# A hybrid decoder layer on one core: the GDN samples' side work queued behind the casts of the states, their decay on ScalarE and additions made wider, and key norms five columns at a time

## The chip, the core and the metric

One NeuronCore of a Trainium2 chip. The time is device microseconds for one execution of the whole program, from 512 prompt tokens and 8 sequences of 8 sample tokens to all eight outputs.

## The reference, cut

```python
def _layer(x, s_gla, s_gdn, conv_buf, ...):
    h = _rmsnorm(x, ln_g)
    proj = h @ w_in                                   # 2048 x 18480
    (q_a, k_a, v_a, lr_a, gate_a, qkv_b, beta_b, dec_b, gate_b, m_a, m_b) = split(proj)
    ...
    o_a, s_gla_new = _gla_chunked(q_a, k_a, v_a, log_alpha, s_gla)       # 4 heads, 256 x 512 states
    y_a = (rmsnorm(o_a) * silu(gate_a)) @ w_br_a
    qkv, conv_new = _causal_conv(qkv_b, conv_buf, conv_w)
    q_b, k_b, v_b = split(silu(qkv))
    q_b, k_b = _l2norm(q_b) * GDN_DK ** -0.5, _l2norm(k_b)
    o_b, s_gdn_new = _gdn_chunked(q_b, k_b, v_b, g, beta, s_gdn)         # 16 heads, 128 x 128 states
    y_b = (rmsnorm(o_b) * silu(gate_b)) @ w_br_b
    return x + (sigmoid(m_a) * y_a + sigmoid(m_b) * y_b) @ w_out, s_gla_new, s_gdn_new, conv_new

def step(s, inp):                                     # of _gdn_chunked, one chunk
    ...
    sol = triangular_solve(eye + m, [v * beta, k * beta * exp(gh)])      # -> u, w
    v_new = u - w @ s
    o = (q * exp(gh)) @ s + qk @ v_new
    s = s * exp(g_last) + k_end.T @ v_new
```

The layer runs twice, on the prompt with zero states and on the samples with states that are loaded; then a last RMSNorm. For the samples each of 16 GDN heads has eight states of 128 x 128.

## The kernel before, in words

Every projection is a row of blocks of 128 output columns over all 576 tokens. A block takes 96 matmuls on TensorE in two halves (256 prompt tokens; 256 prompt and 64 sample tokens): weights and tokens are split into a high and a low part, and three products are added. The weights of the block after the next are loaded, and those of the next are cut while a block runs: the high part `hi` by ScalarE (L249), the low part `lo` by VectorE (L252). All else is side work: generators that issue a piece, name a pause and are taken up again when TensorE's matmuls have gone on by so much (`Seq`, L41). TensorE's order is the order of writing. On the other engines the framework's scheduler orders instructions by its own estimate of when they can start; each engine then runs its queue strictly in that order. `S.marks` holds instructions behind which, on their own engine, everything is queued that a later step of side work issues; before the change it holds only the last cast of weights on ScalarE.

The change touches two places.

*The key heads* (`key_task`, L927, 16 heads, some 250 us): the key rows' squares are summed per token into `ss`, four columns of 128 tokens and one of 64 sample tokens. VectorE makes from them the write strengths and the factors of the end-of-chunk keys, and GpSimd the norms `sqk`, once for the four columns and once for the fifth (L957 to L965).

*The GDN samples* (L1515 to L1679), which run beside eleven blocks of merge gates (`mth`, L1008, is their tanh). Per head h:

- `gdn_sample_load` (L1518) loads the eight states `Sbd` (512 KB, five buffers) and the head's small tiles; the load of h + 2 is issued at the start of head h.
- `gdn_sample_prep` (L1535) cuts keys and queries into `kqp` and the states into `Shl`: high part by ScalarE (L1551), low part by VectorE (L1552), each in two halves of four states. It is issued in head h - 1, right after `zs`.
- `gdn_sample` (L1556): eight `ksq` matmuls; ScalarE copies their low-part columns to `ksqe` (L1567); eight additions on VectorE make `ks_` and `qs_`; `zs` (L1577); matmul `nps`; its copy `nns` (L1584); `kw` (ScalarE and VectorE) goes to HBM (`d_kw`, L1595).
- `gdn_sample_end` (L1600): matmul `ops`, the output `os`, its squares `jks` (L1610), its factor `rss` (L1611 to L1613, the last a power on GpSimd), its scaling by GpSimd (L1614); `kr` comes back from HBM (L1616); transpose `op2`, product with the gate, store; GpSimd spreads `kr` into `bd` (L1626); two matmuls `sps2`, after each of which VectorE updates four states in place, `Sbd * decay + sps2` (L1635); the states go out (L1638).

All DMAs are issued by SP in one queue. There, in steady work, stand per head: the states of h - 3 out, `d_kw` of h, the load of `Sbd` for h + 2, `d_ob`, `kr`, seven small loads. Five buffers mean that the load for h + 2 waits until the states of h - 3 are out.

The matmul of `sps2` for head h comes about three heads after its `ksq`; the second of its two stands, for half of the heads, just behind the `ksq` of head h + 3.

Of the kernel before, what the change touches and what calls it, by code (L numbers as in the profile page):

```python
# [7 lines left out]
F32 = mybir.dt.float32  # L8
F32R = mybir.dt.float32r
U8 = mybir.dt.uint8  # L10
AF = mybir.ActivationFunctionType
ALU = mybir.AluOpType
# [4 lines left out]
P = 128  # L17
# [3 lines left out]
TS = 64  # L21
T = TP + TS
HALVES = ((0, 256), (256, T))
NB = 8
# [3 lines left out]
EPS = 1e-6  # L28
# [75 lines left out]
def build(ctx, tc, nc, x_p, x_s, st_gla, st_gdn, st_conv, ln_g, w_in, w_al, b_al, conv_w,  # L104
# [3 lines left out]
    S = Seq(tc)  # L108
# [44 lines left out]
    halfc = cg.tile([P, 1], F32, name="halfc")  # L153
# [5 lines left out]
    def build_masks(maskb):  # L159
        G.memset(maskb, 0.0)  # L160
        mp = maskb[:, 0:P]
        G.affine_select(out=mp, in_=mp, pattern=[[1, P]], compare_op=ALU.is_ge,
                        fill=NEG, base=0, channel_multiplier=-1)
        ms2 = maskb[:, P:P + TS]
        G.affine_select(out=ms2, in_=ms2, pattern=[[1, TS]], compare_op=ALU.is_ge,
                        fill=NEG, base=0, channel_multiplier=-1)
        ms = ms2.rearrange("p (b s) -> p b s", s=LS)
        G.affine_select(out=ms, in_=ms, pattern=[[-LS, NB], [0, LS]], compare_op=ALU.is_ge,
                        fill=NEG, base=0, channel_multiplier=1)
        V.tensor_scalar(cmask, maskb, -1.0, None, ALU.is_ge)  # L170
# [6 lines left out]
    def chunks():  # L177
        return ((P, 0, 4), (TS, 4, 5))
# [748 lines left out]
    def key_task(pk, h, ext, exs, lst, ready):  # L927
# [14 lines left out]
                         bias=nghc[:, c, h:h + 1])  # L942
        A.activation(W[0:TS, TP:T], R[0:TS, TP:T], AF.Exp, bias=nghc[0:TS, 4, h:h + 1])
        yield 10.0
        ss = pk.tile([P, 5], F32, name="ssk", tag="ssk")
        jk = pk.tile([P, P], F32, name="jk", tag="jk", bufs=1)
        kp = big("kp")
        for c in range(4):
# [5 lines left out]
        A.activation(jk[0:TS], kps[0:TS, 0:P], AF.Square, accum_out=ss[0:TS, 4:5])  # L954
        tb = pk.tile([P, 5], F32, name="tb", tag="tb")
        ck = pk.tile([P, 5], F32, name="ck", tag="ck")
        for n, s, e in chunks():  # L957
            V.tensor_scalar(tb[0:n, s:e], ss[0:n, s:e], EPS, None, ALU.add)
            V.reciprocal(ck[0:n, s:e], tb[0:n, s:e])
            V.tensor_tensor(out=bti[0:n, h, s:e], in0=ck[0:n, s:e], in1=btc[0:n, s:e, h],  # L960
                            op=ALU.mult)
            V.tensor_tensor(out=ck[0:n, s:e], in0=bti[0:n, h, s:e], in1=ekc[0:n, s:e, h],
                            op=ALU.mult)
            G.tensor_tensor(out=sqk[0:n, h, s:e], in0=tb[0:n, s:e],
                            in1=halfc[0:n].broadcast_to([n, e - s]), op=ALU.pow)  # L965
        ke = pk.tile([P, 5, P], F32, name="ke", tag="ke")
        for c in range(4):
            V.tensor_scalar(ke[:, c], kp[:, c * P:(c + 1) * P], ck[:, c:c + 1], None, ALU.mult)
# [51 lines left out]
    def k_open():  # L1020
        cp_open()
        px = pool(kctx2, "px", side="right")
        lrb, dec, lrs, zt = (px.tile([32, T], F32, name="lrb"), px.tile([16, T], F32, name="dec"),
                             px.tile([96, T], F32R, name="lrs"), px.tile([P, TS], F32, name="zt"))
        SY.dma_start(dec, d_dc)
        SY.dma_start(lrb, d_lr)
        G.memset(lrs.bitcast(F32), 0.0)
        G.memset(zt, 0.0)
        pk = kst["pk"] = pool(kctx, "pk", bufs=2)
        hk = pk.tile([P, 16, 24], F32, name="hisk", bufs=1)  # L1030
        SY.dma_start(hk, d_hi[:, 16:32])
        for j in range(16):
            his[16 + j] = hk[:, j]
        kst["lst"] = (pk.tile([P, 16, 3], F32, name="lstP", bufs=1),
                      pk.tile([P, 16, 24], F32, name="lstS", bufs=1))
        kst["maskb"] = pk.tile([P, P + TS], F32, name="maskb", bufs=1)
        build_masks(kst["maskb"])
        kst["p2c"] = ExitStack()
        kst["p2"] = pool(kst["p2c"], "p2", side="right")
        ev = S.spawn(iter(()), 5.0)  # L1040
        kst["tok"] = S.spawn(token_scalars(kst["p2"], lrb, dec, lrs, zt, ev, kst["colsready"]))
# [493 lines left out]
    def gdn_sample_prep(h, loaded):  # L1535
        pe2 = est["pe2"]
        Sb, kq, vk, ua, gt = loaded

        kqp = est["kqp"][h % 2]
        kq4 = kq.rearrange("p a (j x) -> p a j x", j=2)  # L1540
        for a in range(2):
            for j in range(2):
                src = kq4[:, a, j].rearrange("p (b s) -> p b s", s=LS)
                hi, lo = (kqp[:, 512 * j + 64 * a + o:512 * j + 64 * a + o + 544].rearrange(
                    "p (b x) -> p b x", x=136)[:, :, 0:LS] for o in (0, 32))
                A.copy(hi, src)
                V.tensor_tensor(out=lo, in0=src, in1=hi.bitcast(F32), op=ALU.subtract)
        sh = pe2.tile([P, NB, 2, P], F32R, name="Shl", tag="Shl")
        for j in range(2):
            bs = slice(4 * j, 4 * j + 4)  # L1550
            A.copy(sh[:, bs, 0], Sb[:, bs])  # L1551
            V.tensor_tensor(out=sh[:, bs, 1], in0=Sb[:, bs], in1=sh[:, bs, 0].bitcast(F32),  # L1552
                            op=ALU.subtract)
        return sh

    def gdn_sample(h, loaded, sh, ahead):  # L1556
        pe, pe2 = est["pe"], est["pe2"]
# [7 lines left out]
        kj = ksq.rearrange("p (j a v) -> p j a v", j=2, a=2)  # L1565
        e = pe2.tile([P, 2, P], F32, name="ksqe", tag="ksqe", bufs=1)
        A.copy(e, kj[:, :, 1])  # L1567
        ks_ = pe2.tile([TS, P], F32, name="ks_", tag="ks_")
        qs_ = pe2.tile([TS, P], F32, name="qs_", tag="qs_")
        for out, o in ((ks_, 0), (qs_, 64)):  # L1570
            for j in range(2):
                r = slice(32 * j, 32 * j + 32)
                V.tensor_tensor(out=out[r], in0=kj[o:o + 32, j, 0], in1=e[o:o + 32, j],
                                op=ALU.add)
                V.tensor_tensor(out=out[r], in0=kj[o + 32:o + 64, j, 0], in1=out[r], op=ALU.add)
        zs = pe2.tile([TS, P], F32, name="zs", tag="zs")
        V.scalar_tensor_tensor(out=zs, in0=ks_, scalar=neghc[0:TS, 4, h:h + 1],  # L1577
                               in1=vk[:, 0], op0=ALU.mult, op1=ALU.add)
# [2 lines left out]
        np_ = chn("nps")  # L1581
        mm(np_[0:TS, 0:P], ua[:, 0], zs)
        nn = pe2.tile([TS, P], F32, name="nns", tag="nns")
        V.tensor_copy(nn, np_[0:TS, 0:P])  # L1584
        kw = pe2.tile([TS, 3, 256], F32R, name="kw", tag="kw")
        A.copy(kw[:, 0, 0:P], vk[:, 1])
        A.copy(kw[:, 2, 0:P], vk[:, 1])
# [6 lines left out]
        for j in range(2):  # L1594
            SY.dma_start(d_kw[h].rearrange("(x r) j c -> x r j c", r=3)[:, :, j],  # L1595
                         kw[32 * j:32 * j + 32].bitcast(F32))
        S.spawn(gdn_sample_end(h, loaded, nn, qs_), 3.0)
        yield 3.4

    def gdn_sample_end(h, loaded, nn, qs_):  # L1600
# [10 lines left out]
        V.tensor_scalar(rs, sqq[0:TS, h, 4:5], P * EPS, P * EPS * EPS, ALU.mult, ALU.add)  # L1611
        V.scalar_tensor_tensor(out=rs, in0=so, scalar=1.0 / P, in1=rs, op0=ALU.mult, op1=ALU.add)
        G.tensor_tensor(out=rs, in0=rs, in1=nhalf[0:TS], op=ALU.pow)  # L1613
        G.tensor_scalar(o_, o_, rs, None, ALU.mult)  # L1614
        kr = pe2.tile([96, 2, 256], F32R, name="kr", tag="kr")
        SY.dma_start(kr.bitcast(F32), d_kw[h])  # L1616
        yield 8.0
# [12 lines left out]
        for j in range(2):  # L1630
            sp = big("sps2")
            mm(sp, kr[:, j, 0:P], bd[:, j].rearrange("p g v -> p (g v)"))
            for g in range(4):
                b = j * 4 + g
                V.scalar_tensor_tensor(out=Sb[:, b], in0=Sb[:, b], scalar=elb[:, h, 4 + b:5 + b],  # L1635
                                       in1=sp[:, g * P:(g + 1) * P], op0=ALU.mult, op1=ALU.add)
            yield 1.0
        SY.dma_start(n_gdn_s[0, :, h].rearrange("b d v -> d b v"), Sb)  # L1638

# [34 lines left out]

    def m1_close():
        S.join()
        ectx.close()

    add_m(NM1, pre=m1_open, post=m1_close)  # L1679
# [338 lines left out]
```

## Time and profile before

| | |
|---|---|
| median of 3 runs | 2873.26 us (2872.47 to 2873.99) |
| the profiled execution | 2873.5 us, span 2871.8 us |
| TensorE busy | 2800.1 us (98%) |
| VectorE, ScalarE, GpSimd busy | 1758.8, 1032.6, 420.9 us (61%, 36%, 15%) |
| mean granted TensorE clock | 0.987 of full speed |

Engines are called PE (TensorE matmul), PEld (its weight loads), DVE (VectorE), ACT (ScalarE), POOL (GpSimd) and SP; SPq is SP's queue of DMA issues. Times are in us from the span's start. A matmul's duration includes its way through the array, so consecutive ones overlap; what one costs is the distance between starts. In brackets behind an instruction stands how long its engine was idle before it and what ended that. A wait for several things is put down to the last one.

### The profile page before, as it was taken

Reading aid. Unit: us, or ns where it says so; the run is one execution under the profiler, and the core shown is the slowest. Engines: PE = TensorE matmul, PEld = TensorE weight load, DVE = VectorE, ACT = ScalarE, POOL = GpSimd, SP = SyncE. Lnnn points to the kernel's source line nnn. Section 1 sums busy time; section 2 is a strip of 40 time slices with the busy share of each in tenths; the row PEclk is TensorE's granted clock in tenths of the full one; section 3 lists DMA queues with packets and bytes.
Section 4 is the critical chain, followed back from the end, with each engine's and each line's share of the span. In section 5 each row is a group of like instructions: output and inputs, shape, how many; then the busy total and the mean of one; then the engine's idle time right before and its main releaser. Section 6 shows DMA issues by size and latency. Waiting matters only on the chain.

```text
span 2871.8 us, 50272 instructions
## 1 busy us (share of the span) xinstructions
PE 2800.1 (98%) x19894; PEld 2669.6 (93%) x19894; DVE 1758.8 (61%) x3578; ACT 1032.6 (36%) x2305; POOL 420.9 (15%) x605
## 2 busy tenths in 40 slices
PE   8999999999999999999999999997799999999998
PEld 7999999989999999999999999997689888999886
DVE  7677665766568888634666666657654664533323
ACT  5444444655423232333333333333333332322222
POOL 2000000542101010101222222212210000111111
PEclk9999999999999999999999999998899999999999
DMA  6333334555653333535454444456666887644422
GB/s 165 118 114 122 126 121 140 155 176 166 171 123 80 105 102 94 146 95 141 122 136 122 126 134 122 116 147 174 171 208 198 269 289 245 185 128 125 168 75 96
DMA packets 550057, 417.33 MB, mean 145 GB/s; under 512 B 78389, under 2 KB 475397, under 8 KB 547893
## 3 DMA queue, kind: packets, MB, share of 16 engines
q1 hardware_dynamic: 549822, 414.13, 50.1%
q8 instruction: 156, 2.56, 0.4%
q14 instruction: 79, 0.65, 0.1%
HBM read 313.65 MB, written 100.40 MB: 144 GB/s over the span
## 4 chain that ended last, share of the span: by engine, by line
PE 70%; DVE 4%; issue 2%; POOL 1%; DMA 1%; ACT 1%; SPq 0%; POOLq 0%; DVEq 0%; ACTq 0%
PE mm L115 53%; PE oacc L115 7%; PE opd L115 1%; PE sps L115 1%; DVE tmp L899 1%; DVE lo L252 1%; PE ksq L115 1%; PE sp L115 1%; PE qk L115 0%; PE spd L115 0%; DVE nt L902 0%; PE ksp L115 0%; POOL bd L1626 0%; PE yp L115 0%; PE kk L115 0%
## 5 line engine op out<-in xcount | busy, mean ns | idle before, releaser
L115 PE MATMUL mm<-hh,hi 128*128 128x320 f32 (+2 forms) x3928 | 1183.8, 304 | 0.3 <-DVE qd L1241 0.3
L115 PE MATMUL mm<-hl,hi 128*128 128x320 f32 (+2 forms) x3928 | 1152.6, 296 | 0.0
L115 PE MATMUL mm<-hh,lo 128*128 128x320 f32 (+2 forms) x3928 | 1104.2, 296 | 1.2 <-DVE lo L252 0.9
L115 PEld LDWEIGHTS mm<-hh,hi 128*128 128x128 f32 x3928 | 746.6, 190 | 9.0 <-issue 3.8
L115 PEld LDWEIGHTS mm<-hl,hi 128*128 128x128 f32 x3928 | 746.0, 190 | 1.9
L115 PEld LDWEIGHTS mm<-hh,lo 128*128 128x128 f32 x3928 | 725.2, 190 | 1.9 <-DVE lo L252 1.2
L252 DVE TENSOR_TENSOR lo<-raw,hi 128x512 fp32r<-128x512 f32 x624 | 435.5, 719 | 264.6 <-ACT hi L249 263.2
L249 ACT CAST hi<-raw 128x512 fp32r<-128x512 f32 x628 | 359.4, 619 | 562.0 <-PE mm L115 460.7
L115 PE MATMUL mm<-lb,hi 128*128 128x320 f32 (+1 forms) x1024 | 211.3, 300 | 0.0
L115 PE MATMUL mm<-ra,hi 128*128 128x320 f32 (+1 forms) x1024 | 202.3, 294 | 0.0
L115 PEld LDWEIGHTS mm<-lb,hi 128*128 128x128 f32 x1024 | 165.1, 189 | 17.6 <-issue 14.9
L115 PE MATMUL oacc<-hi,m 128*128 128x512 f32 x540 | 171.1, 390 | 0.0
L115 PEld LDWEIGHTS mm<-ra,hi 128*128 128x128 f32 x1024 | 163.6, 188 | 0.0
L115 PE MATMUL mm<-lb,lo 128*128 128x320 f32 (+1 forms) x512 | 151.2, 295 | 0.0
L115 PE MATMUL mm<-ra,lo 128*128 128x320 f32 (+1 forms) x512 | 150.6, 294 | 0.0
L115 PE MATMUL mm<-tl,hi 128*128 128x288 f32 x544 | 146.8, 295 | 0.0
L115 PE MATMUL mm<-th,hi 128*128 128x288 f32 x544 | 146.7, 297 | 0.0
L899 DVE TENSOR_TENSOR tmp<-nt 128x1 f32<-128x1 f32 (+36 forms) x163 | 131.5, 807 | 3.0
L115 PEld LDWEIGHTS oacc<-hi,m 128*128 128x128 f32 x540 | 101.4, 188 | 25.2
L854 DVE SCALAR_TENSOR_TENSOR acc<-ext,cwT,acc 128x600 f32<-128x600 f32 x144 | 121.1, 841 | 0.9 <-ACT acc L852 0.6
L379 DVE TENSOR_TENSOR lo<-raw,hi 128x1024 fp32r<-128x1024 f32 x68 | 83.0, 1221 | 55.7 <-ACT hi L378 54.2
L115 PE MATMUL oacc<-lo,m 128*128 128x512 f32 x300 | 117.0, 392 | 0.0
(905 smaller groups left out, 3835.9 us busy)
## 6 DMA issues: line engine op xcount, KB each, us to landing
raw<-in_w_in SPq DMA_DIRECT2D x144, 1024.0 KB, 6.2
raw<-in_w_br_b SPq DMA_DIRECT2D x16, 1024.0 KB, 6.0
Sb<-in_state_gla SPq DMA_DIRECT2D x32, 512.0 KB, 5.8
out<-Sb SPq DMA_DIRECT2D x32, 512.0 KB, 3.1
raw<-in_w_br_a SPq DMA_DIRECT2D x16, 1024.0 KB, 6.1
raw<-in_w_out SPq DMA_DIRECT2D x16, 1024.0 KB, 5.1
Sbd<-in_state_gdn SPq DMA_DIRECT2D x16, 512.0 KB, 6.8
out<-Sbd SPq DMA_DIRECT2D x16, 512.0 KB, 3.3
```

The costliest lines, as they stand in the source:

```text
L115: PE.matmul(out, lhsT, rhs, start=start, stop=stop, **kw)
L249: hc = A.copy(hi, raw)
L252: cut = eng.tensor_tensor(out=lo, in0=raw, in1=hi.bitcast(F32), op=ALU.subtract)
L379: last_split[0] = V.tensor_tensor(out=lo, in0=src, in1=hi.bitcast(F32), op=ALU.subtract)
L854: V.scalar_tensor_tensor(out=acc, in0=ext[:, i:i + 600], scalar=cw(i), in1=acc, op0=ALU.mult, op1=ALU.add)
L899: V.tensor_tensor(out=tv, in0=nt[:, cs, c0:i], op=ALU.mult, in1=nt[:, c0:i, i:i + 1].rearrange("p j o -> p o j").broadcast_to([P, m, i - c0]))
```

## The change

Five edits. (1) `gdn_sample_prep` puts the last cast of the states on ScalarE and its low half on VectorE into `S.marks`: what later steps of side work issue on these engines is queued behind them, until the samples are done. (2) The decay of the states leaves the update: ScalarE multiplies each state in place (`gdn_sample_decay`), right after `kw`, and the update is one addition of 512 columns per `sps2`. (3) The high- and low-part columns of `ksq` are added for all 128 rows in one instruction, and the four additions of 32 rows that are left read SBUF alone. (4) The copy `nns` and the scaling of `os` go to ScalarE. (5) The key norms are handled for all five columns at once; the parts of the fifth column that no sample fills, and `ss`, are cleared beforehand by GpSimd.

```diff
-        ss = pk.tile([P, 5], F32, name="ssk", tag="ssk")
+        ss = kst["ss"][h % 2]
...
-        for n, s, e in chunks():
-            V.tensor_scalar(tb[0:n, s:e], ss[0:n, s:e], EPS, None, ALU.add)
-            V.reciprocal(ck[0:n, s:e], tb[0:n, s:e])
-            V.tensor_tensor(out=bti[0:n, h, s:e], in0=ck[0:n, s:e], in1=btc[0:n, s:e, h],
-                            op=ALU.mult)
-            V.tensor_tensor(out=ck[0:n, s:e], in0=bti[0:n, h, s:e], in1=ekc[0:n, s:e, h],
-                            op=ALU.mult)
-            G.tensor_tensor(out=sqk[0:n, h, s:e], in0=tb[0:n, s:e],
-                            in1=halfc[0:n].broadcast_to([n, e - s]), op=ALU.pow)
+        V.tensor_scalar(tb, ss, EPS, None, ALU.add)
+        V.reciprocal(ck, tb)
+        V.tensor_tensor(out=bti[:, h], in0=ck, in1=btc[:, :, h], op=ALU.mult)
+        V.tensor_tensor(out=ck, in0=bti[:, h], in1=ekc[:, :, h], op=ALU.mult)
+        G.tensor_tensor(out=sqk[:, h], in0=tb, in1=halfc.broadcast_to([P, 5]), op=ALU.pow)
...
+        kst["ss"] = [pk.tile([P, 5], F32, name=f"ssk{i}", bufs=1) for i in range(2)]
+        for t_ in kst["ss"] + [btc, ekc]:
+            G.memset(t_, 0.0)
...
-            A.copy(sh[:, bs, 0], Sb[:, bs])
-            V.tensor_tensor(out=sh[:, bs, 1], in0=Sb[:, bs], in1=sh[:, bs, 0].bitcast(F32),
-                            op=ALU.subtract)
+            S.marks["sA"] = A.copy(sh[:, bs, 0], Sb[:, bs])
+            S.marks["sV"] = V.tensor_tensor(out=sh[:, bs, 1], in0=Sb[:, bs],
+                                            in1=sh[:, bs, 0].bitcast(F32), op=ALU.subtract)
         return sh
+
+    def gdn_sample_decay(h, Sb):
+        for b in range(NB):
+            A.activation(Sb[:, b], Sb[:, b], AF.Copy, scale=elb[:, h, 4 + b:5 + b])
...
         A.copy(e, kj[:, :, 1])
+        V.tensor_tensor(out=e, in0=kj[:, :, 0], in1=e, op=ALU.add)
...
-                r = slice(32 * j, 32 * j + 32)
-                V.tensor_tensor(out=out[r], in0=kj[o:o + 32, j, 0], in1=e[o:o + 32, j],
-                                op=ALU.add)
-                V.tensor_tensor(out=out[r], in0=kj[o + 32:o + 64, j, 0], in1=out[r], op=ALU.add)
+                V.tensor_tensor(out=out[32 * j:32 * j + 32], in0=e[o:o + 32, j],
+                                in1=e[o + 32:o + 64, j], op=ALU.add)
...
-        V.tensor_copy(nn, np_[0:TS, 0:P])
+        A.copy(nn, np_[0:TS, 0:P])
...
+        gdn_sample_decay(h, Sb)
         S.spawn(gdn_sample_end(h, loaded, nn, qs_), 3.0)
...
-        G.tensor_scalar(o_, o_, rs, None, ALU.mult)
+        A.activation(o_, o_, AF.Copy, scale=rs)
...
-            for g in range(4):
-                b = j * 4 + g
-                V.scalar_tensor_tensor(out=Sb[:, b], in0=Sb[:, b], scalar=elb[:, h, 4 + b:5 + b],
-                                       in1=sp[:, g * P:(g + 1) * P], op0=ALU.mult, op1=ALU.add)
+            half_ = Sb[:, 4 * j:4 * j + 4].rearrange("p b v -> p (b v)")
+            V.tensor_tensor(out=half_, in0=sp, in1=half_, op=ALU.add)
...
         S.join()
+        S.marks.pop("sA"), S.marks.pop("sV")
```

The lines of the kernel after are some four lower than before in the key heads and one to three different in the samples (`Shl` L1550 and L1551, `nns` L1586, decay L1557, update L1637). TensorE's matmuls stand in the same order in both, and so do SP's DMAs of the samples but for the places of three around head 14.

On ScalarE before, around the casts of the states of head 11 (`jks` is that of head 10):

```order
L249 CAST hi<-raw 128x512 x4
L1610 ACTIVATE jks,sos<-os 64x128
L1586 CAST kw<-vks 64x128
L1587 CAST kw<-vks 64x128
L1551 CAST Shl<-Sbd 128x4x128 x2
L1546 CAST kqp_21683<-kqs 128x4x8 x4
L1567 COPY ksqe<-ksq 128x256
L1590 CAST kw<-nns 64x128
```

On ScalarE now, around the casts of the same states (`ksqe` and `nns` are those of head 10, `os` that of head 9):

```order
L1570 COPY ksqe<-ksq 128x256
L1545 CAST kqp_21594<-kqs 128x4x8 x4
L1617 ACTIVATE os<-os,rss 64x128
L249 CAST hi<-raw 128x512
L1004 ACTIVATE mth<-mm 128x320
L249 CAST hi<-raw 128x512 x3
L1550 CAST Shl<-Sbd 128x4x128 x2
L1586 COPY nns<-nps 64x128
L1588 CAST kw<-vks 64x128
L1589 CAST kw<-vks 64x128
L1592 CAST kw<-nns 64x128
L1593 CAST kw<-nns 64x128
```

The casts moved from behind `jks` of head 10 to ahead of its `nns`; the four `hi` and a `mth` stand ahead of them.

On VectorE before, around the low halves of the states of head 11 (`os` and the first `rss` are of head 10; the `rss` of L1611 is of head 12):

```order
L1609 TENSOR_TENSOR os<-ops,qs__23443 64x128
L1621 TENSOR_TENSOR oTs<-op_23566,gts 128x64
L1635 SCALAR_TENSOR_TENSOR Sbd<-Sbd,elb,sps_23574 128x128
L1612 SCALAR_TENSOR_TENSOR rss<-sos,rss 64x1
L1635 SCALAR_TENSOR_TENSOR Sbd<-Sbd,elb,sps_23574 128x128 x3
L252 TENSOR_TENSOR lo<-raw,hi 128x512 x2
L1588 TENSOR_TENSOR kw<-vks,kw 64x128
L252 TENSOR_TENSOR lo<-raw,hi 128x512
L1611 TENSOR_SCALAR rss<-sqq 64x1
L1552 TENSOR_TENSOR Shl<-Sbd,Shl 128x4x128 x2
```

On VectorE now, around the low halves of head 13 (`zs` and the rows behind `Shl` are of head 12, but the first Sbd is the second half of the update of head 9, the next one the first half of head 10):

```order
L1579 SCALAR_TENSOR_TENSOR zs<-ks__23673,neghc,vks 64x128
L1546 TENSOR_TENSOR kqp_21594<-kqs,kqp_21594 128x4x8 x4
L252 TENSOR_TENSOR lo<-raw,hi 128x512 x4
L1551 TENSOR_TENSOR Shl<-Sbd,Shl 128x4x128 x2
L1637 TENSOR_TENSOR Sbd<-sps_23694,Sbd 128x512
L1590 TENSOR_TENSOR kw<-vks,kw 64x128
L1594 TENSOR_TENSOR kw<-nns,kw 64x128
L1637 TENSOR_TENSOR Sbd<-sps_23775,Sbd 128x512
L1612 TENSOR_TENSOR os<-ops,qs__23674 64x128
L1614 TENSOR_SCALAR rss<-sqq 64x1
```

The low halves moved ahead of `os`, `rss` and `kw` of the head before; behind them stands the second half of the update of the head four before.

## Rows read from the trace of the kernel before

**Rows 1.** Busy time by stretches: us, busy us per engine, PEclk, DMA share, GB/s.

```profile
1600.00:1897.00 297.00, 296.56 (x2334) 290.66 (x2333) 176.59 (x459) 97.87 (x262) 66.22 (x122) 1.00 0.47 127
...
1902.00:2104.00 202.00, 165.36 (x1025) 150.36 (x1025) 148.88 (x469) 72.77 (x250) 49.34 (x56) 0.88 0.62 167
...
2131.00:2400.00 269.00, 269.00 (x1790) 242.59 (x1788) 154.12 (x276) 94.08 (x178) 10.49 (x9) 1.00 0.82 255
```

**Rows 2.** Waits from 1880 to 2130: us in total, times, longest us.

```profile
PE ksq L115 <- DVE Shl L1552: 32.0, 9, 6.6
...
ACT jks L1610 <- DVE os L1609: 18.8, 9, 4.0
...
ACT Shl L1551 <- DMA uas<-d_At: 6.2, 1, 6.2
...
PE nps L115 <- DVE zs L1577: 4.6, 4, 2.0
```

**Rows 3.** Timeline: start, us, engine, line, instruction, count, idle before it.

```profile
1942.04 1.10 PE L115 MATMUL ksq<-Shl,kqp 128*128 128x256 f32 x8
...
2043.05 0.31 ACT L1610 ACTIVATE jks<-os 64x128 f32<-64x128 f32 x1
...
2043.74 1.14 ACT L1551 CAST Shl<-Sbd 128x512 fp32r<-128x512 f32 x2
...
2044.38 2.52 POOL L1614 TENSOR_SCALAR os<-os,rss 64x128 f32<-64x128 f32 x1
...
2046.93 0.15 DVE L1611 TENSOR_SCALAR rss<-sqq 64x1 f32<-64x1 f32 x1 [0.51 <-POOL os L1614]
2047.01 3.04 DVE L1552 TENSOR_TENSOR Shl<-Sbd,Shl 128x512 fp32r<-128x512 f32 x2
...
2049.51 2.07 PE L115 MATMUL ksq<-Shl,kqp 128*128 128x256 f32 x8 [6.63 <-DVE Shl L1552]
```

**Rows 4.** Chain of waits from 1880 to 2130: start, us, what.

```profile
1887.06 11.76 PE mm L115 x90
...
2084.54 0.36 PE nps L115 x2
...
2087.74 0.23 PE sps L115
...
2089.61 0.95 PE ksq L115 x8
```

**Rows 5.** Groups by line and shape: count, busy us, mean ns, idle before.

```profile
L1635 DVE SCALAR_TENSOR_TENSOR Sbd<-Sbd,elb,sps 128x128 f32<-128x128 f32 x120 | 35.9, 341 | 20.8 <-PE sps L115 20.1
...
L1577 DVE SCALAR_TENSOR_TENSOR zs<-ks__22961,neghc,vks 64x128 f32<-64x128 f32 x1 | 2.0, 1971 | 0.0
...
L1573 DVE TENSOR_TENSOR qs__22323<-ksq,ksqe 32x128 f32<-32x128 f32 x2 | 0.6, 285 | 0.0
...
L1925 DVE TENSOR_TENSOR r<-oacc,r 128x512 f32<-128x512 f32 x16 | 11.0, 692 | 40.9 <-PE oacc L115 40.9
...
L1177 DVE TENSOR_TENSOR ktl<-kdtp,kth 128x256 fp32r<-128x256 f32 x16 | 6.8, 422 | 1.4 <-ACT kth L1176 1.4
...
L1551 ACT CAST Shl<-Sbd 128x512 fp32r<-128x512 f32 x32 | 18.5, 614 | 6.2 <-DMA uas<-d_At 6.2
...
L941 ACT ACTIVATE W<-R,nghc 128x128 f32<-128x128 f32 x64 | 20.9, 392 | 17.2 <-POOL R L936 8.4 <-issue 7.7 <-POOL sqk L964 1.1
```

**Rows 6.** DMA issues from 1897 to 2131: count, KB each, us to landing.

```profile
Sbd<-in_state_gdn SPq DMA_DIRECT2D x15, 512.0 KB, 6.8
out<-Sbd SPq DMA_DIRECT2D x15, 512.0 KB, 3.3
```

**Rows 7.** Waits of SP's queue from 1897 to 2131: us, times, longest.

```profile
SPq L1521 <- DMA out<-Sbd: 9.7, 9, 2.6
```

**Rows 8.** Key heads: a wait (500 to 800), and line L958, min/median/max ns.

```profile
PE kp L125 <- DVE kT L858: 5.9, 2, 4.1
...
L958 DVE TENSOR_SCALAR tb<-ssk x32: 111/150/937, 524.4 to 771.5; 128x4 f32<-128x4 f32 x16, 64x1 f32<-64x1 f32 x16
```

## The prediction, made before the change was run

> **What bounds the kernel now.** I read the busy time by stretches first [rows 1]. TensorE is busy 296.56 of 297 us before the GDN samples; in the stretch of the samples it is busy only 165.36 of 202 us, at a granted clock of 0.88. So nearly the whole program is bound by TensorE, and what the edits around the samples can win lies in these 202 us, between the first `ksq` and that of the last of 16 heads.
>
> What would they take if TensorE never waited? Its order is the same in both programs, and counting it gives 804 block matmuls (414 of 256 columns, 390 of 320), 15 groups of eight `ksq`, 30 `nps` and `ops`, 26 `sps2` and 14 transposes. At full clock 90 block matmuls take 11.76 us, eight `ksq` 0.95, `nps` 0.36, `sps2` 0.23 [rows 4]; with `ops` priced as `nps` and the transposes as `sps2` that is 105 + 14.3 + 10.8 + 9.2 = 139 us, or 9.3 per head. The other 63 us are lost: 36.6 of no work (202 less 165.4) and 26 of work at the lower of the two clock levels (165.4 less 139).
>
> The waits say at what [rows 2]: 32.0 us in nine waits of `ksq` for the low half of the state, 4.6 for `zs`. One of the nine can be followed in [rows 3]. ScalarE casts the next state only behind `jks`, which needs `ops` of the head before, and `ops` stands just ahead of `ksq` on TensorE. The cast is done at 2044.9; then VectorE stands at L1611, the `rss` of two heads on, until GpSimd lets the old `rss` go (its `os` took 2.52 us), and the low half starts at 2047.01. TensorE had nothing for 6.63 us, and its `ksq` then took 2.07 instead of 0.95. ScalarE's `jks` alone waited 18.8 us in nine waits [rows 2].
>
> None of this is in the first heads: the fifth `ksq` is at 1942.04 [rows 3], 10.0 us per head from 1902. The other eleven intervals take 162 us, 14.7 each.
>
> **The change, part by part.**
>
> *The queueing.* With the two marks, `jks`, L1611 and the rest of a head's side work stand behind the next head's casts on both engines, as the order shows. This takes away what ends 32.0 us of waits and, with them, most of the 26 us of slow clock: 58 us at most, 63 with the `zs` waits gone too.
>
> *VectorE's work per head.* The state's update was eight instructions of 0.341 us, 2.7; now two additions of 512 columns. The nearest row with one PSUM and one SBUF input is the residual's, 0.692 [rows 5]: 1.4. The eight additions of 32 rows at 0.285 make 2.3; now one of 256 columns (nearest `ktl`, 0.422 [rows 5]) and four small ones at 0.285 or down to half of it, 1.0 to 1.6. The copy `nns` (priced like them, 0.3) leaves. VectorE gains about 2.5 us of the 9.3 that worked 148.88 / 16 = 9.3 [rows 1]: it stops being as full as TensorE. On the path `ksq` to `zs` four additions of 0.285 (1.1) become five instructions of 1.0 to 1.6, so it is between 0.1 shorter and 0.5 longer; in TensorE's order 27 to 32 rows, nearly all block matmuls of 0.13 (11.76 / 90), stand between `ksq` and `nps`, some 3.5 us, which covers it.
>
> *ScalarE's work per head.* Eight decays of 128 columns with a scale from a tile: nearest is `W`, 0.392 [rows 5], and 0.3 if they overlap as the two Shl casts do (1.14 for two of 0.614 [rows 3, 5]), so 2.4 to 3.1; `nns` and the scaling of `os` at 0.3 each. 72.77 / 16 = 4.5 [rows 1] becomes 7.5 to 8.2 of 9.3. It fits, and nothing on TensorE waits for a decay. But `nns` now stands behind the casts of the next state on ScalarE, with `kw` and its DMAs behind it; who waits is `ops`, and then `ksq`.
>
> *The load of the states*, the term that I let decide. SP's order is the same: out of head h-3, `d_kw` of h, load of h+2, and that load takes the buffer (one of five) that head h-3 gives back. Out needs the second half of the update, and on VectorE that half now stands behind the low half of state h+1 for six heads (5, 6, 7, 9, 10, 11; the VectorE piece of the new order shows one). So a round closes: state lands, two casts (1.14), second low half (0.7, priced like the residual's addition, which has its 512 columns), addition (0.69), out to landing (3.3), load to landing (6.8) [rows 3, 5, 6], five hand-overs of 0.1: 13.1 us per head against TensorE's 9.3. SP waited for out to land 9.7 us in nine waits already [rows 7], without a cost then, since heads took 14.7.
>
> *Sum.* Five intervals go at this round's 13.1 (states 9 to 12 and 13 to 15), the other six at the 10.0 of the first heads: 125.5 us. 162 less 125.5 is 36.5. Ends: TensorE's own 9.3 in all eleven, 102, saves 60; the round in all eleven, 144, saves 18, and with 0.6 more for collisions 11.
>
> *The key norms.* Ten small VectorE instructions per head become four, six of about 0.15 fewer [rows 8], and one power on GpSimd. TensorE waits for VectorE in that stage 5.9 us in two waits [rows 8]; everything else there is covered by block matmuls. A gain of up to 5.9, a loss of as much if the reordered queue puts a conv behind something else; both waits hang on the row of decays that comes by DMA, so I take 0. The four memsets lie on GpSimd at the stage's opening, under block matmuls: 0.
>
> *A rule against the change.* In the trace `zs`, with two SBUF inputs, took 1.97 us in one head [rows 5] while GpSimd was at `bd`, and the additions from PSUM beside it 0.285. The four small additions now read two SBUF inputs each, ahead of `zs`. The Trainium skill (GPSIMD Engine Reference, Specifications) says that GpSimd shares its SBUF interfaces with VectorE, with contention where a VectorE instruction has two SBUF inputs; by that rule all five can be held, and the trace agrees in the one `zs`. By the rows alone: a hit of 1.6 us (1.97 less some 0.3) on a path with some 1 us to spare costs under 1 us in a head, 0 to 7 in all. I take 0 in the sum; it is in the third case below.
>
> **The rivals.**
>
> *The load round does not bite.* For it: ScalarE's casts of the states waited for a DMA once, at the start [rows 2], and 6.8 was read at a DMA share of 0.62 [rows 1, 6]. Then all eleven go at 10.0: 110, 52 saved, 2821.
>
> *It bites everywhere*, or the casts stay late for another reason: in the new order `mth` and four `hi` still stand ahead of the state casts at each change of block, and those wait for TensorE itself. With the collisions above: all eleven at 13.1, 18 saved, 2855.
>
> *Slower.* Faster heads need the same bytes in less time. If this makes the load land late, the round is all there is, and VectorE's relief does not matter. It decides from 14.7 per head, that is a landing of 8.4 us in every head instead of 6.8; at 9.8 a head takes 16.1, 177 for 162, and the time is 2888. Against it: in the next stretch the DMA moves 255 GB/s at a share of 0.82 and TensorE is busy throughout [rows 1].
>
> *The marks hold nothing that matters.* They bind only what is written in later steps; `hi`, `mth` and the loads are not bound. If these ended the waits, all stays at 2873. Against it: `jks` and L1611 are the last in [rows 3], and both have moved.
>
> **How the numbers follow.** The profiled execution took 2873.5 us with a span of 2871.8; the median of the three runs, 2873.26, is 0.2 below, which I neglect. 2873.5 less 36.5 is 2837. Chances: this forecast 0.49, no round 0.25, round everywhere 0.16, slower 0.06, unchanged 0.04. The range leaves out a tenth on either side: from 2816 (eleven intervals near TensorE's own 9.3) to 2862 (the round with collisions everywhere). Faster by over 0.2%, which is what a measurement can tell here, is the first three, 0.90; within it 0.04; slower 0.06.
>
> **What would show it.** Right: the samples' stretch shrinks from 202 to about 165 us (40 + 125.5); `ksq` waiting for Shl falls below 12 us; in the late heads `ops` waits for `nns`, ScalarE's cast of the state waits for the DMA that brings it, SP's wait for out grows; VectorE's busy time per head falls by 2 to 3 us and ScalarE's grows by 3; heads are 13 us apart late and 10 early; other stretches stay. Wrong: if `ksq` starts stay 10 us apart to the end, the load round was no bound; if they are over 14 apart with the casts waiting for loads, it is a worse one than what was removed; if the wait is at `nps` for `zs`, it was the SBUF collisions.

## The result, and the profile after

| | before | after |
|---|---|---|
| median | 2872.86 us (4 runs) | 2842.07 us (2840.4 to 2843.82, 4 runs) |
| ratio | | 0.9896, 95% interval 0.9884 to 0.9908 |
| profiled span | 2871.8 us | 2838.7 us |

The kernel became 30.8 us faster; the forecast was 2837, its range 2816 to 2862. The profiled executions are 33.1 us apart, and three places hold all of it. The start of the first and of the last `ksq` of each kernel mark them (timeline of TensorE, after: start, duration, instruction, idle before it):

```profile
1898.09 2.04 PE L115 MATMUL ksq<-Shl,kqp 128*128 128x256 f32 x8 [2.88 <-issue]
...
1939.93 1.10 PE L115 MATMUL ksq<-Shl,kqp 128*128 128x256 f32 x8
...
2073.83 1.10 PE L115 MATMUL ksq<-Shl,kqp 128*128 128x256 f32 x8
```

Before, these stood at 1901.67, 1942.04 [rows 3] and 2103.68. So 3.6 us were won ahead of the samples, 26.3 between the first and the last `ksq` (202.0 to 175.7), and 3.2 behind it (768.1 to 764.9). The busy time by stretches, after (us; busy us per engine; PEclk, DMA share, GB/s):

```profile
500.00:780.00 280.00, 275.28 (x2072) 271.08 (x2071) 182.48 (x434) 154.28 (x433) 88.37 (x140) 0.99 0.58 169
1898.00:2074.00 176.00, 153.45 (x1026) 139.09 (x1027) 121.42 (x327) 111.64 (x391) 34.77 (x40) 0.96 0.70 189
2074.00:2101.00 27.00, 27.00 (x194) 25.67 (x194) 12.00 (x30) 11.22 (x36) 7.16 (x8) 1.00 0.75 207
```

and of the two stretches of before that [rows 1] doesn't have:

```profile
500.00:780.00 280.00, 271.40 (x2046) 267.03 (x2045) 186.76 (x495) 154.07 (x433) 102.20 (x156) 0.99 0.56 166
...
2104.00:2131.00 27.00, 27.00 (x174) 25.75 (x173) 11.70 (x36) 4.55 (x12) 8.03 (x9) 0.89 0.69 189
```

In the samples TensorE's idle time fell from 36.6 us to 22.6 (176.0 less 153.45) and the granted clock rose from 0.88 to 0.96. The clock also explains the 3.2 us behind the last `ksq`: the same 27 us hold 194 matmuls in place of 174. Before, that stretch still ran partly at the lower of the two clock levels (0.50), after a stretch with many gaps; now it runs at full clock. The low spell (before, columns as above):

```profile
2103.60:2109.20 5.60, 5.52 (x26) 5.52 (x27) 3.25 (x11) 0.37 (x1) 3.10 (x3) 0.50 0.84 232
```

Part of this is chance of the profiled execution. In the twelve other changed kernels below the same stretch took between 766.2 and 767.1 us, in that with the old norms, whose samples are those of the kernel after, 766.2. So 1 to 2 of the 3.2 us are usual and the rest was not seen again.

The waits of the samples, after (engine, line, waited for: us, times, longest):

```profile
ACT Shl L1550 <- DMA Sbd<-in_state_gdn: 21.0, 7, 6.3
...
PE ops L115 <- ACT nns L1586: 11.4, 7, 3.0
...
PE nps L115 <- DVE zs L1579: 8.6, 9, 2.6
...
ACT jks L1613 <- DVE os L1612: 6.6, 5, 2.7
```

The 32.0 us in which `ksq` waited for `Shl` [rows 2] are gone altogether. In their place `ops` waits for `nns`, which stands behind the casts of the next states, and those casts wait for their DMA. Not all of the 21.0 us is new: the first of the seven waits stands ahead of the first `ksq`, and before there was one like it (6.2 us in [rows 2], there with `uas` as the last DMA to land):

```profile
1895.74 0.62 ACT L1550 CAST Shl<-Sbd 128x512 fp32r<-128x512 f32 x1 [6.26 <-DMA Sbd<-in_state_gdn]
```

The other six, 14.8 us, are those of the late heads. SP's queue waits longer for the stores than in [rows 7]:

```profile
SPq L1520 <- DMA out<-Sbd: 14.0, 11, 2.3
```

The chain that ended last shows the new bound as a circle (after; start, us, what):

```profile
1961.17 3.26 DMA out<-Sbd
...
1964.44 7.03 DMA Sbd<-in_state_gdn
...
1971.50 0.63 ACT Shl L1550
...
1972.15 0.56 DVE Shl L1551
...
1972.80 0.64 DVE Shl L1551
...
1973.84 1.11 DVE Sbd L1637 x2
1974.95 3.34 DMA out<-Sbd
```

A store lands, the load behind it lands, two casts, two low halves, the update that stands behind them, and the next store: 13.8 us from store to store. It is the longest of three in a row in this chain; the one ahead of it took 11.4 us, the one behind it 9.1.

### The profile page after: what moved, and what is told of

It is laid out like the page before. It is cut to its first block, busy times and chain, and to the rows that moved or that the text cites. A ratio compares the mean times of both kernels' runs of the same rounds, so it can differ in the third digit from the quotient of the medians.

```text
span 2838.7 us, 50151 instructions
## 1 busy us (share of the span) xinstructions
PE 2785.4 (98%) x19894; PEld 2656.7 (94%) x19894; DVE 1724.3 (61%) x3354; ACT 1076.2 (38%) x2465; POOL 390.6 (14%) x577
## 4 chain that ended last, share of the span: by engine, by line
PE 70%; DMA 3%; DVE 3%; issue 1%; ACT 1%; SPq 0%; POOL 0%; DVEq 0%; POOLq 0%; ACTq 0%
PE mm L115 53%; PE oacc L115 7%; DMA Sbd<-in_state_gdn 1%; DMA out<-Sbd 1%; PE sps L115 1%; PE opd L115 1%; DVE tmp L899 1%; PE sp L115 1%; PE qk L115 1%; PE spd L115 0%; PE ksp L115 0%; DVE nt L902 0%; PE kk L115 0%; DVE lo L252 0%; PE yp L115 0%
## 5 line engine op out<-in xcount | busy, mean ns | idle before, releaser
L378 ACT CAST hi<-raw 128x1024 fp32r<-128x1024 f32 x68 | 71.4, 1051 | 125.1 <-PE mm L115 70.2
```

What stands on the lines that cost most here:

```text
L378: S.marks[A] = A.copy(hi, src)
```

## The experiments

Intervals of differences between two kernels below are the root of the summed squares of the half-widths of their ratios, times 2873 us. Two things limit what the traces of single kernels can tell. The framework's scheduler orders a changed kernel anew, so with some edits (six buffers, the decay elsewhere, `nns` on VectorE) much of the order on ScalarE and VectorE differs, not the edited lines alone. And each trace is one execution. The kernel with the old norms shows by how much executions differ: its samples are those of the kernel after, in the same order on ScalarE, VectorE and GpSimd, and yet `nps` waits 5.8 us for `zs` instead of 8.6 and the casts of the late heads 12.3 for their DMA instead of 14.8 (`ops` 11.8 for `nns` instead of 11.4, SP 14.7 for the stores instead of 14.0). So a difference of 3 us in one of these waits shows nothing by itself.

**The load round.** Six buffers for the states instead of five.

```diff
-        Sb = pe2.tile([P, NB, P], F32, name="Sbd", tag="Sbd", bufs=5)
+        Sb = pe2.tile([P, NB, P], F32, name="Sbd", tag="Sbd", bufs=6)
-        kq = pe2.tile([P, 2, TS], F32, name="kqs", tag="kqs", bufs=4)
+        kq = pe2.tile([P, 2, TS], F32, name="kqs", tag="kqs", bufs=2)
...
-        vk = pe2.tile([TS, 2, P], F32, name="vks", tag="vks", bufs=4)
+        vk = pe2.tile([TS, 2, P], F32, name="vks", tag="vks", bufs=3)
...
-        jk = pe2.tile([TS, P], F32, name="jks", tag="jks")
+        jk = pe2.tile([TS, P], F32, name="jks", tag="jks", bufs=1)
```

> The kernel after with six buffers for the states instead of five (room for it: two buffers for kqs, three for vks, one for jks, none of which any engine waited for). Theory (the load round bounds the late heads): SP no longer waits for the states of h-3 to be out (14.0 us in 11 waits after), ScalarE's cast waits for the DMA of the states under 5 us (21.0 in 7 after), the ten late heads fall from 12.3 us each to about 10.5, the time is 2822 to 2830. Rival (the loads only seem to be the limit: hi and mth of the block of gates stand ahead of the casts on ScalarE and wait for TensorE, so that nns and ops are late in any case): the wait moves from the DMA to TensorE or to nns, the time stays at 2842, within 3.

Measured: 2825.31 us (2824.92 to 2829.31), ratio 0.9835 (0.9821 to 0.9848), 17 us less than the kernel after, within 5. Its busy time between the first and the last `ksq`, its waits and SP's:

```profile
1897.00:2061.00 164.00, 151.77 (x1024) 137.85 (x1025) 120.04 (x327) 113.17 (x395) 37.45 (x40) 0.97 0.73 195
```

```profile
PE nps L115 <- DVE zs L1579: 5.2, 5, 2.1
...
PE ops L115 <- ACT nns L1586: 4.2, 3, 2.4
...
ACT Shl L1550 <- DMA Sbd<-in_state_gdn: 1.6, 3, 0.8
```

```profile
SPq L1520 <- DMA out<-Sbd: 3.4, 5, 1.7
```

The casts' wait for the DMA in the late heads fell from 14.8 to 1.6 us (the wait ahead of the first `ksq` stayed, 6.0), SP's for the stores from 14.0 to 3.4, and `ops` waited 4.2 instead of 11.4. The round was the bound. The eleven late heads took 11.1 us each (122.0 in all) instead of 12.2 (133.9): 0.6 more than was expected here. What is left is not spread evenly; the first five of the eleven took 10.2 us each, the last six 11.8:

```profile
1939.00:1990.20 51.20, 49.27 (x340) 44.39 (x339) 43.06 (x112) 36.94 (x132) 12.95 (x15) 1.00 0.77 206
1990.20:2061.00 70.80, 61.96 (x410) 56.12 (x410) 49.55 (x134) 46.04 (x159) 18.09 (x18) 0.95 0.77 204
```

This is the lowest median measured.

**The marks.** Taken out of the kernel after, and put alone into the kernel before.

```diff
-            S.marks["sA"] = A.copy(sh[:, bs, 0], Sb[:, bs])
-            S.marks["sV"] = V.tensor_tensor(out=sh[:, bs, 1], ...
+            A.copy(sh[:, bs, 0], Sb[:, bs])
+            V.tensor_tensor(out=sh[:, bs, 1], ...
```

> The kernel after without the two marks, all other edits kept. Theory (the queueing ends the waits): ksq waits for the low half of the states again, 15 to 32 us in 6 to 9 waits, with jks ahead of the cast on ScalarE; 2855 to 2870. Rival (the relief of VectorE by the decay on ScalarE and the wider additions is what did it): ksq waits under 8 us, 2842 to 2848.

> The kernel before with the two marks and nothing else. Theory (the queueing ends the waits, then the load round with VectorE's own 9.3 us per head is the bound): ksq waits under 12 us, 2843 to 2858. Rival (relief of VectorE did it): stays within 5 of 2873. A second rival: with VectorE as full as before, rss, os and the update now stand behind the low half, the states go out later, the loads land later, and it is slower than before, above 2878.

Without the marks it took 2862.8 us (2862.11 to 2866.58), with the marks alone 2854.22 (2852.87 to 2856.88). The waits of the first:

```profile
PE ksq L115 <- DVE Shl L1551: 30.8, 9, 5.8
```

and of the second:

```profile
ACT Shl L1551 <- DMA Sbd<-in_state_gdn: 15.7, 5, 5.8
...
PE ops L115 <- DVE nns L1584: 15.0, 6, 4.6
```

All the relief of VectorE leaves the wait for `Shl` where it was (30.8 us after 32.0), though the four other edits together won 10 us (2862.8 for 2873.2); the marks alone end it and already uncover the load round. They are worth 19 us alone and 20 to 21 on top of the rest, of 30.8.

**One mark of the two.** The mark on VectorE out, that on ScalarE kept.

```diff
-            S.marks["sV"] = V.tensor_tensor(out=sh[:, bs, 1], ...
+            V.tensor_tensor(out=sh[:, bs, 1], ...
```

> The kernel after without the mark on VectorE (the one on ScalarE stays). In the new order the updates and the rss of the next head then stand ahead of the low half of the states again. Theory A (the mark on VectorE costs more than it brings, since it puts the update, and with it the store and the load of the states, behind the low half): SP's wait for the stores falls under 10 us (14.0 after), 2834 to 2840. Theory B (both marks are needed: the low half stands behind rss, which waits for os, and behind updates that wait for sps2 on TensorE): ksq waits for the low half again, 5 us or more in all, and it is 2845 to 2855.

Measured: 2836.28 us (2834.76 to 2840.71), 6 less than after, within 5.5.

```profile
ACT Shl L1550 <- DMA Sbd<-in_state_gdn: 10.9, 5, 4.7
...
PE ops L115 <- ACT nns L1586: 8.6, 6, 2.5
...
PE ksq L115 <- DVE Shl L1551: 0.3, 1, 0.3
```

With the rest of the change in place, the mark on ScalarE alone ends the waits of `ksq`: 0.3 us are left. (No run has the mark on VectorE alone.) The one on VectorE puts the update behind the low half and so into the load round; without it SP waits 9.3 us for the stores instead of 14.0. The casts wait 10.9 us instead of 14.8, which is hardly less than the 12.3 of another execution of the same samples, and the profiled execution was the slowest of the four, 2840.71 us, as long as that of the kernel after. So the gain of 6 us, barely clear of its interval, rests on the times; how it comes about is shown in part only, by SP's wait.

**The key norms** as before in the kernel after (the whole of the fifth edit undone).

> The kernel after with the key norms as before (four columns and the fifth apart, no memsets). Theory A (the first sample's ksq came 3.6 us earlier in the profile after because TensorE no longer waits 2.6 us for the decays and less for kT in the key heads): 2844 to 2847, and the wait of kps for the decays is back. Theory B (as predicted, the norms are worth 0, the 3.6 us are chance of the queue's order): within 1.5 of 2842.

Measured: 2848.26 us (2842.95 to 2850.25); the difference of 4 us by the ratios (0.9909 against 0.9896) is not clear of its interval of 5. The traces are clearer. The first `ksq` came at 1903.57 here, at 1901.67 and 1902.59 in the two other kernels with the old norms, and between 1896.4 and 1899.4 in all eleven kernels that have the new ones. A wait that was there before came back:

```profile
PE kps L125 <- DVE ab L791: 2.6, 1, 2.6
```

and `kp` waits 5.8 us for `kT` (5.9 in [rows 8], 4.4 after). By the traces the norms are worth about 4 us.

**The decay back on VectorE**, with everything else kept.

```diff
-            V.tensor_tensor(out=half_, in0=sp, in1=half_, op=ALU.add)
+            for g in range(4):
+                b = j * 4 + g
+                V.scalar_tensor_tensor(out=Sb[:, b], in0=Sb[:, b], scalar=elb[:, h, 4 + b:5 + b],
+                                       in1=sp[:, g * P:(g + 1) * P], op0=ALU.mult, op1=ALU.add)
...
-        gdn_sample_decay(h, Sb)
```

> The kernel after with the decay back in the update on VectorE (eight instructions of 0.34 us in a head in place of two of 0.68), ScalarE without the eight decays. Theory A (with the marks VectorE's load still counts, through zs and through the update that the store waits for; marks alone with the old VectorE work took 2854, of which the norms are 4 to 6): 2845 to 2851. Theory B (the load round takes what VectorE gives, so its relief is worth nothing): 2840 to 2843.

Measured: 2835.33 us (2832.91 to 2837.08), ratio 0.9868 (0.9852 to 0.9885): 8 us less than after by the ratios, within 6. Neither theory had this sign. So the second edit, which was to relieve VectorE, costs time with five buffers. The trace doesn't say by what: `nps` waits 5.1 us for `zs` and `ops` 9.5 for `nns`, both less than after but within what executions differ by, the casts 17.3 for their DMA, which is not less. What does change clearly is that ScalarE has slack again, 22.6 us of waiting for `ksq` instead of 5.7. The next two runs ask whether the decays cost by making ScalarE late.

**The decay at another place on ScalarE**, behind the copy `ksqe` of the next head.

```diff
-        gdn_sample_decay(h, Sb)
...
-        A.copy(e, kj[:, :, 1])
+        ei = A.copy(e, kj[:, :, 1])
+        if h:
+            with tc.issue_after(ei.ins):
+                gdn_sample_decay(h - 1, est["last"])
+        est["last"] = Sb
```

> The kernel after with the eight decays of a head kept on ScalarE, but queued behind the copy ksqe of the next head, so that they stand ahead of the next hi and casts and no longer between kw and ksqe. With the decay back on VectorE the time was 2835.3, 6.7 below the kernel after. Theory A (the decays cost because of where they stand: 2.46 us ahead of jks and ksqe when the casts came late, which ends in zs): ScalarE waits for ksq again (over 15 us, 5.7 after), nps waits for zs under 6 us (8.6 after), 2833 to 2838. Theory B (it is ScalarE's time as such, casts and hi come later by as much): 2840 to 2845.

Measured: 2843.46 us (2843.0 to 2845.06). Theory A falls: ScalarE does wait for `ksq` again (15.1 us in eight waits, 5.7 after), but `nps` waits 9.0 us for `zs` and `ops` 11.8 for `nns`, as after. Taking the decays away from in front of `jks` and `ksqe` gained nothing.

> Both steps that gained, together: six buffers for the states (2825.3) and the decay back on VectorE (2835.3). Theory A (two different waits, the load round and the queue on ScalarE ahead of ksqe): the gains of 17 and 7 add for the most part, 2817 to 2822. Theory B (with the load round gone, VectorE's work counts again, so the decay is better placed on ScalarE): 2825 to 2832.

Six buffers and the decay on VectorE (both diffs above): 2830.66 us (2828.26 to 2832.89), 5 more than with six buffers alone by the ratios, not clear of its interval of 6: the gains do not add. `nps` waits 9.0 us for `zs` (5.2 with six buffers) and `ops` 3.3. With the load round gone there is no gain left in taking the decay off ScalarE. That fits a ScalarE that is late only because the casts are, but no run shows that link by itself; why the decays cost time stays open.

**The copy `nns` and the additions** as before, each alone in the kernel after.

```diff
-        A.copy(nn, np_[0:TS, 0:P])
+        V.tensor_copy(nn, np_[0:TS, 0:P])
```

> The kernel after with the copy nns on VectorE, where it was before. nns stands behind the next head's casts on either engine; on VectorE the low half comes some 0.65 us after the cast on ScalarE. Theory A (ops waits for nns because it stands behind the casts of the states): the waits of ops stay and grow, 13 to 22 us for 11.4 in the profile after, the time is 2843 to 2850. Theory B (ScalarE is the engine that is late, VectorE has time): ops waits under 8 us, 2836 to 2840.

```diff
-        V.tensor_tensor(out=e, in0=kj[:, :, 0], in1=e, op=ALU.add)
...
-                V.tensor_tensor(out=out[32 * j:32 * j + 32], in0=e[o:o + 32, j],
-                                in1=e[o + 32:o + 64, j], op=ALU.add)
+                r = slice(32 * j, 32 * j + 32)
+                V.tensor_tensor(out=out[r], in0=kj[o:o + 32, j, 0], in1=e[o:o + 32, j], op=ALU.add)
+                V.tensor_tensor(out=out[r], in0=kj[o + 32:o + 64, j, 0], in1=out[r], op=ALU.add)
```

> The kernel after with the additions of ksq as before (eight of 32 rows, each with one operand in PSUM). Theory A (the wide addition and the four small ones on SBUF save VectorE 0.5 to 1.1 us in a head ahead of zs): nps waits longer for zs than 8.6 us, 2843 to 2848. Theory B (the small additions, with two operands in SBUF, are held by bd on GpSimd in seven heads, 0.6 to 2.1 us for two, and narrow ones that read PSUM are not): 2838 to 2841. Between, no difference.

Measured: 2844.71 us (2842.83 to 2846.58) and 2844.67 (2840.83 to 2847.38), both no different from 2842.07 by their intervals. With `nns` on VectorE `ops` waits 15.4 us for it instead of 11.4, as theory A had it. `nps` waits 5.2 us for `zs` there and 5.8 with narrow additions, which is theory B's direction for those; but 5.8 is also what another execution of the kernel after's own samples showed, and nothing of it reaches the time. The scaling of `os` on ScalarE, the other half of the fourth edit, was not tried alone.

**GpSimd's `bd`.** One of the two spreads of a head left out.

```diff
-        for j in range(2):
+        for j in range(1):
             G.tensor_tensor(out=bd[:, j], op=ALU.mult, ...
...
-            mm(sp, kr[:, j, 0:P], bd[:, j]...
+            mm(sp, kr[:, j, 0:P], bd[:, 0]...
```

> The kernel after with one of the two spreads of kr on GpSimd left out (the first half serves both matmuls sps2, so the new states are wrong in half of the state heads' slots). In the profile after, VectorE's instructions with two operands in SBUF took 0.6 to 2.2 us instead of 0.18 to 0.28 while bd ran (2.03 us for two), some 14 us in all, and zs held TensorE 8.6 us in nine waits. Theory A (bd on GpSimd holds VectorE, and that ends the waits for zs): the long instructions are about 1.0 us at most, the waits of nps fall to 3 to 6 us, 2836 to 2840. Theory B (they fall on time that VectorE has to spare, the load round is the bound): 2841 to 2844.

Measured: 2840.06 us (2835.01 to 2843.14), not different from after: 3 us less by the ratios, with an interval of 5.5. The longest of the held instructions shrank with `bd` (`kqp` from 2.23 to 1.24 us) and `nps` waited 3.1 us for `zs` instead of 8.6, as theory A had it, but `ops` waited 12.8 for `nns` and the casts of the late heads 17.8 for their DMA. The median lies between the ranges of the two theories, so the time does not decide between them; it shows that half of `bd` is worth 9 us at the most.

**`zs` first**, with six buffers: the preparation of the next head queued behind `zs` (`zi` in the diff).

```diff
-        ahead()
+        with tc.issue_after(zi.ins):
+            ahead()
```

> Six buffers for the states (2825.3) with the preparation of the next head (kqp, the casts of its states and their low halves) queued behind zs of this head on VectorE and so out of its way. In the profile with six buffers nps still waited for zs 5.2 us in five waits and ops for nns 4.2 in three. Theory A (what stands ahead of zs in VectorE's queue, kqp and the low halves, is what zs waits for): nps waits under 2.5 us, 2818 to 2824. Theory B (zs waits for ksqe on ScalarE and for bd, and the low halves that are now later hold ksq instead): within 3 of 2825 or slower.

Measured: 2827.42 us (2824.08 to 2831.01), as with six buffers alone. Theory A was right on the wait (1.6 us instead of 5.2) and wrong on the time: `ksq` waits 1.7 us for `kqp` and `sps2` 1.7 for `bd` instead, and what is left is spread over many waits of a microsecond.

## Why the prediction was right, point by point

*What bounds, and the queueing.* Right. The waits of `ksq` were to fall below 12 us and fell to nothing; the marks were to be the cause and are, the one on ScalarE by itself. But the wait that was followed in [rows 3] was not queueing alone. The first of its two low halves took 2.44 us, where 0.68 is usual, while GpSimd was at `bd`; 1.8 of the 6.63 us went there. (GpSimd's `os` ahead of it, 2.52 us in [rows 3], takes 0.61 as a rule; three `lo` of VectorE ran beside it.) The low halves of all heads before (min/median/max ns), and GpSimd:

```profile
L1552 DVE TENSOR_TENSOR Shl<-Sbd,Shl x32: 673/684/2440, 1900.0 to 2103.5; 128x512 fp32r<-128x512 f32 x32
```

```profile
2046.87 2.03 POOL L1626 TENSOR_TENSOR bd<-kr,bm 96x512 fp32r<-96x512 f32 x2
```

*The load round.* Right as a mechanism, and each sign that was named for it came: `ops` waits for `nns`, the casts for their DMA, SP longer for the stores. 13.1 us was the forecast of a round in each of five heads; 13.8 is the longest shown above, with shorter ones beside it. Its heads were not those named: the intervals 9 to 12 and 13 to 15 took 12.4 us on average, the other six 12.0.

*The sum.* 26.3 us came in the samples where 36.5 were forecast; this is the term that was mis-sized. The first four intervals took 41.8 for 40, the eleven late ones 133.9 for 125.5. Six buffers part the two terms of the late heads. Without the round they took 122.0 us where eleven at 10.0 make 110, so 12 more; the round then added 11.9 where five times the 3.1 between 10.0 and 13.1 makes 15.5. By the heads that were named the same: those five took 61.9 for 65.5, the other six 72.0 for 60.0. So the step that failed is "the other six at the 10.0 of the first heads". TensorE's own work is not the reason, since the third and the fourth interval, which already hold two `sps2` each, took 9.7 and 10.0 us. With six buffers the first five late heads came near it (10.2); the last six (11.8) lost 8.8 us in waits, of `ops` for `nns` (4.2), of `nps` for `zs` (2.1) and of `sps2` for the update (1.9) above all, and ran at a granted clock of 0.95. What makes `nns` and `zs` late there no run isolates.

*ScalarE's work per head.* "It fits, and nothing on TensorE waits for a decay" was too short. ScalarE's busy time rose from 4.9 to 7.4 us a head (111.64 / 15), the forecast was 7.5 to 8.2, and eight decays took 2.4 to 2.5, at the lower end. But at a busy share of 63% ScalarE, whose order is fixed, is late whenever an entry at the head of its queue is. The timeline of one head in the kernel after, ScalarE:

```profile
1994.97 1.14 ACT L1550 CAST Shl<-Sbd 128x512 fp32r<-128x512 f32 x2 [3.30 <-DMA Sbd<-in_state_gdn]
1996.02 0.25 ACT L1586 COPY nns<-nps 64x128 f32<-64x128 f32 x1
...
1996.98 2.45 ACT L1557 ACTIVATE Sbd<-Sbd,elb 128x128 f32<-128x128 f32 x8
...
1999.63 0.35 ACT L1570 COPY ksqe<-ksq 128x256 f32<-128x256 f32 x1
...
2007.04 0.38 ACT L1004 ACTIVATE mth<-mm 128x256 f32<-128x256 f32 x1 [3.33 <-PE mm L115]
2007.32 1.13 ACT L1550 CAST Shl<-Sbd 128x512 fp32r<-128x512 f32 x2
```

The cast waited 3.30 us for its DMA, and everything behind it moved by that. The last two rows show the second rival's other reason, too: `mth` waits 3.33 us for TensorE with the next casts behind it. It is there, but with six buffers most of the wait for `nns` went, though `mth` then waited 33.3 us in all for TensorE instead of 21.3.

*VectorE's work per head.* From 9.9 us to 8.1 (121.42 / 15): 1.8 less, 2 to 3 were forecast. The updates were priced right (0.68 each for 0.69).

*The key norms.* Taken as 0 within 5.9, measured about 4 as a gain. The 0 rested on the two waits for `kT`; the wait of `kps` for `ab`, 2.6 us, was not in the account, and it is the larger part of what left. Why both waits shrank is not shown.

*The stretch behind the samples* was to stay and gave 3.2 us, as the lower level of the clock lasted into it before and not in this execution after; 1 to 2 us by the other kernels.

*The shared SBUF interfaces* (the Trainium skill, GPSIMD Engine Reference, Specifications), 0 to 7 us and taken as 0. The trace agrees with the rule, as the last section shows. The reading from which the bound came was too small: before the change not one `zs` was held but four, beside `bd` each time, and three of these four end a wait of `nps` (the fourth such wait came behind a `kqp` that took 2.62 us beside `bd`). One of the four:

```profile
2065.75 1.85 DVE L1577 SCALAR_TENSOR_TENSOR zs<-ks__23759,neghc,vks 64x128 f32<-64x128 f32 x1
```

```profile
2065.42 2.03 POOL L1626 TENSOR_TENSOR bd<-kr,bm 96x512 fp32r<-96x512 f32 x2
```

In all, `bd` held VectorE for 13 us in the samples before and 17 after. That the block matmuls between `ksq` and `nps` cover the path to `zs` did not hold: `zs` holds TensorE 8.6 us in nine waits (5.8 in the other execution of these samples) where it held it 4.6 in four, and that was one of the signs named against the forecast. Halving `bd` moved the time by less than its interval, so 0 is not contradicted, but it is known to some 5 us only.

That the total was only 5 us off is luck: the terms that were left at 0, the norms and the clock behind the samples, gave back 6.8 of the 10.2 that the samples fell short in the profiled execution.

## What to carry to other kernels

When a wait is removed, follow the buffers of the engine that is now faster: the circle of store, load, cast and update could be read from a few rows of the trace of before, and one more buffer was worth more than half of what the whole change was. Don't price the late heads of a loop by its first ones: even without the round the last six took 11.8 us, and 10.0 was the price. Work is not free on an engine because that engine has time on average: the decay, moved to ScalarE at 4.9 us of work in a head, cost 8 us with five buffers, and why is still open. So undo each part of a bundle alone, and profile one unchanged piece of code twice, to see which differences between traces mean something.

## What the runs showed of the hardware

Beside GpSimd's `bd` some of VectorE's instructions with two operands in SBUF hardly move. The kernel after, VectorE and GpSimd:

```profile
2000.01 0.42 DVE L1571 TENSOR_TENSOR ksqe<-ksq,ksqe 128x256 f32<-128x256 f32 x1
2000.35 2.23 DVE L1546 TENSOR_TENSOR kqp<-kqs,kqp 128x32 fp32r<-128x32 f32 x1
2002.61 0.59 DVE L1576 TENSOR_TENSOR ks__23189<-ksqe 32x128 f32<-32x128 f32 x2
```

```profile
2000.50 2.03 POOL L1629 TENSOR_TENSOR bd<-kr,bm 96x512 fp32r<-96x512 f32 x2
```

`kqp` takes 0.18 us as a rule; here it took 2.23 and ended 0.05 us after `bd` did (2000.50 + 2.03). In 19 places of the samples `kqp`, the small additions or `rss` took half as long again as usual or more, 17 us in all over their usual times, and in each of the 19 `bd` ran beside them. Six others with two operands in SBUF overlapped with `bd` and took their usual time. Of the instructions that read one operand from PSUM 23 overlapped with `bd`, and none was held: the additions and updates among them never took over 0.43 and 0.69 us.
